# A reworked chain at the output product and the latents, and a head in pairs of row tiles

## The chip, the cores and the metric

The kernel runs on one core of a Trainium2 chip. The metric is device time in microseconds of one execution; lower is better. The engines named below are TensorE (PE), VectorE (DVE), ScalarE (ACT), GpSimd (POOL) and SyncE (SP, which issues transfers).

## The reference

One inference step of a decoder trunk with two layers, for 256 prompt tokens and 8 sample tokens (264 columns in all) with D = 1024. A layer is a SwiGLU block, a mixer and a second SwiGLU block, each behind an RMS norm. The mixer joins a gated short convolution with latent attention:

```python
yp = yp + 0.5 * swiglu(rmsnorm(yp, norm_ffn1[l]), w_ffn1_gate[l], w_ffn1_up[l], w_ffn1_down[l])
h = rmsnorm(yp, norm_mix[l])
b_g, u, qn, qp, ckv, kpe = mixer_project(h, w_in[l], q_a_norm[l], w_q_b[l], kv_a_norm[l], pos_p)
conv_y = b_g * short_conv(u_hist, conv_w[l], SEQ)
attn_o = prompt_mla(qn, qp, ckv, kpe, w_kv_b[l])
yp = yp + mixer_output(conv_y, attn_o, gn_conv[l], gn_attn[l], w_o[l])
yp = yp + 0.5 * swiglu(rmsnorm(yp, norm_ffn2[l]), w_ffn2_gate[l], w_ffn2_up[l], w_ffn2_down[l])
```

`mixer_output` normalises the convolution's 512 features and the attention's 512 features each by its own RMS and multiplies both with `w_o` (1024 x 1024). The sample group does the same with a paged cache of 1024 past positions. The FFN is 2816 wide. All inputs are float32.

## The kernel before

Features lie on the 128 partitions, tokens along the 264 columns, so D = 1024 is 8 tiles of rows, y[:, 0] to y[:, 7]. Every large weight comes as float32 in chunks of 256 columns and 8 row tiles (1 MB, tag "raw", 3 buffers) on SP's queue, and is split per unit of 128 columns into a high half (L231, a copy on ACT to fp32r) and a low half (L233, the rest, on DVE), each in two parts of 4 row tiles. There are 5 buffers for split units. `take()` hands the next split unit to the products, `done()` splits the next one; a chunk whose two units are split frees its buffer for the next load. A product of two split numbers is three matmuls (`mm3`, L250 high x high, L251 high x low, L252 low x high). `behind()` puts the low half on DVE behind the instruction last noted in `after[0]`.

The program is traced in one order, and a planner in the build orders the instructions of each engine by their place in the program and by when they become ready in its own model. So the order on an engine isn't always that of the text.

A norm goes like this: squares are summed in `ssA` or `ssB` over the row tiles; `sums` (L312) reduces that in blocks of 32 on DVE and adds over the partitions with a small matmul (L317); `rsqrt_of` (L298) is eight small operations of DVE; `over_rows` (L319) spreads the result over all rows by a transposition. `finish_y` (L329) makes the high and the low part of the next stage's right side `xg` from y (ACT and DVE) and the square's sum, on GpSimd in the output product except for the last tile.

The head (L995 to L1023) loads y in two halves of 4 row tiles (SP and ACT queue), the first weight chunk in two pieces and the next two chunks whole. Fifty matmuls on zeros or ones warm TensorE up; then xg for tiles 0 to 3, the first parts of units 0 and 1, xg for tiles 4 to 7, the second parts, and the squares, in between units 2 and 3. In the first FFN (`ffn`, `first`) units 0 and 1 (gate) run over all row tiles, then units 2 and 3 (up) with the norm's sums behind their first row tile, into the four "mm" banks of PSUM. Three banks bear the tag "x".

In the mixer (`mixer`) three generators are mixed by hand (ORDER): main (12 products of the projection, which give the convolution's four tiles z, each with high part h and low part lo), prompt (the latents, keys, queries and the eight heads) and sample (the cached attention). `latent` (L574) scales the latent (`ckvf`), splits it on ACT and DVE (`ckh`, `ckl`) and rotates the keys on GpSimd (`kp1`, `kp2`, `kpf`). A head's scores p, and their transposed copy pt, take a buffer of the tag "w" each (`wtile`, 4 buffers). `o_stats` (L933) reduces `ssA` (attention) and `ssB` (convolution) to two factors, `a_spread` (L947) scales and splits the attention's four tiles into `mg`, `c_spread` spreads the convolution's factor, and the output product runs row tile by row tile over four banks at once: row tiles 0 to 3 are the convolution's, 4 to 7 the attention's. `o_finish` (L961) evicts a bank (L963), adds to y (L964), splits the next unit and calls `finish_y`. Tiles 4 to 7 of the output follow one by one, then the second FFN.

## Time and profile before

| what | us |
|---|---|
| median of three runs | 1041.53 (1040.4 to 1047.66) |
| profiled execution | 1033.67 |
| its span, first to last instruction | 1031.9 |
| TensorE busy in the span | 1001.6 (97%) |
| DVE busy | 764.0 (74%) |
| ACT busy | 535.9 (52%) |
| GpSimd busy | 93.9 (9%) |

Times within the profile are counted from the span's start, in microseconds; mean durations are in nanoseconds where a row gives "mean ns". A row of the timeline gives start, duration, engine, line, operation, what it writes and reads, and in brackets how long the engine was idle before it and what ended the wait. An operation's duration overlaps the next one's start: matmuls of 264 columns take 0.28 and start every 0.12.

### The profile page before, as it was taken

The page shows a single profiled execution, that of the slowest core. Times are in us where ns is not written, and L with a number is a line of the kernel's source. Part 1 is how long each engine was busy: PE and PEld are TensorE (multiplying, and loading weights), DVE is VectorE, ACT ScalarE, POOL GpSimd, SP SyncE. Part 2 cuts the span into 40 slices and gives each one's busy share as a digit, 9 for nine tenths or more (in the row PEclk, how much of TensorE's full clock was granted, in tenths as well). Part 3 has the DMA queues.
Part 4 walks back from the last instruction along what each step waited for, and adds up shares of the span by engine and source line. Part 5 has one row for each costly group of instructions (what it writes and reads, how often), then busy time and mean ns, then how long its engine had stood idle before and what let it go on. Part 6 is the DMA issues. An engine that isn't in the chain of part 4 may idle for free.

```text
span 1031.9 us, 21616 instructions
## 1 busy us (share of the span) xinstructions
PE 1001.6 (97%) x8666; PEld 970.5 (94%) x8666; DVE 764.0 (74%) x1753; ACT 535.9 (52%) x1167; POOL 93.9 (9%) x135
## 2 busy tenths in 40 slices
PE   8999999999999999999999999999999899999996
PEld 7999999988788999999999999999878899999996
DVE  6988866689859877756688888566996897777452
ACT  6555445448636555545555555454674555555441
POOL 2110100030402000000001111000322100000000
PEclk9999999999999999999999999999999999999998
DMA  8867665535614755555566667454554265555531
GB/s 276 276 221 242 217 199 193 173 109 194 247 42 164 240 169 191 177 164 188 180 213 232 219 226 230 159 179 154 170 192 178 93 208 191 189 178 174 165 113 43
DMA packets 170787, 190.03 MB, mean 184 GB/s; under 512 B 3936, under 2 KB 163712, under 8 KB 170688
## 3 DMA queue, kind: packets, MB, share of 16 engines
q1 hardware_dynamic: 164048, 167.53, 49.7%
q0 software_dynamic: 5776, 19.49, 5.4%
q10 hardware_dynamic: 864, 1.64, 0.5%
q8 instruction: 68, 1.11, 0.4%
q14 instruction: 31, 0.25, 0.1%
HBM read 187.19 MB, written 1.49 MB: 183 GB/s over the span
## 4 chain that ended last, share of the span: by engine, by line
PE 85%; DVE 10%; ACT 3%; issue 1%; DMA 1%; ACTq 0%; SPq 0%; DVEq 0%
PE mm L250 27%; PE mm L252 27%; PE mm L251 26%; DVE lo L233 4%; PE x L779 1%; DVE y L964 1%; ACT hi L231 1%; DVE xg L332 1%; PE x L830 1%; DMA raw<-in_w_ffn_gate_dram 1%; PE x L694 1%; PE x L681 1%; DVE t L963 1%; ACT qg L635 0%; PE s L658 0%
## 5 line engine op out<-in xcount | busy, mean ns | idle before, releaser
L231 ACT ACTIVATE hi<-raw 128x512 fp32r<-128x512 f32 (+1 forms) x648 | 366.2, 612 | 367.3 <-PE mm L251 245.4
L233 DVE TENSOR_TENSOR lo<-raw,hi 128x512 fp32r<-128x512 f32 (+1 forms) x648 | 417.2, 677 | 112.2 <-ACT hi L231 102.7
L252 PE MATMUL mm<-xg,lo 128*128 128x264 f32 x1648 | 468.0, 284 | 7.1 <-DVE lo L233 7.0
L250 PE MATMUL mm<-xg,hi 128*128 128x264 f32 x1648 | 471.2, 286 | 2.4 <-DVE t L963 1.7
L251 PE MATMUL mm<-xg,hi 128*128 128x264 f32 x1648 | 467.4, 284 | 0.0
L252 PEld LDWEIGHTS mm<-xg,lo 128*128 128x128 f32 x1648 | 308.8, 188 | 10.6 <-DVE lo L233 9.6
L250 PEld LDWEIGHTS mm<-xg,hi 128*128 128x128 f32 x1648 | 310.5, 188 | 5.1 <-ACT hi L231 3.6
L251 PEld LDWEIGHTS mm<-xg,hi 128*128 128x128 f32 x1648 | 310.6, 188 | 0.2
L250 PE MATMUL mm<-act,hi 128*128 128x264 f32 x704 | 200.4, 285 | 0.0
L252 PE MATMUL mm<-act,lo 128*128 128x264 f32 x704 | 199.7, 284 | 0.0
L251 PE MATMUL mm<-act,hi 128*128 128x264 f32 x704 | 199.2, 283 | 0.0
L250 PEld LDWEIGHTS mm<-act,hi 128*128 128x128 f32 x704 | 132.3, 188 | 0.2 <-ACT t L1040 0.2
L252 PEld LDWEIGHTS mm<-act,lo 128*128 128x128 f32 x704 | 132.5, 188 | 0.0
L251 PEld LDWEIGHTS mm<-act,hi 128*128 128x128 f32 x704 | 132.4, 188 | 0.0
L464 POOL DMA_INDIRECT nat<-in_cache_ckv_dram,idx x32 | 33.4, 1044 | 445.7 <-DVE lo L233 189.7
L403 DVE TENSOR_TENSOR t<-mm,t 128x264 f32<-128x264 f32 x88 | 37.6, 427 | 40.1 <-PE mm L252 39.6
L394 DVE TENSOR_TENSOR t<-mm,Rw 128x264 f32<-128x264 f32 x88 | 37.6, 428 | 38.4 <-PE mm L252 38.4
L331 ACT ACTIVATE xg<-y,gains 128x264 fp32r<-128x264 f32 x48 | 24.1, 514 | 29.8 <-DVE y L449 19.1
L397 ACT ACTIVATE t<-t 128x264 f32<-128x264 f32 x88 | 36.3, 412 | 4.4 <-DVE t L394 4.3
L399 DVE SCALAR_TENSOR_TENSOR t<-t,t 128x264 f32<-128x264 f32 x88 | 37.6, 428 | 1.1 <-ACT t L397 1.1
L406 DVE TENSOR_TENSOR act<-t,act 128x264 fp32r<-128x264 f32 x88 | 37.7, 428 | 0.0
L405 ACT ACTIVATE act<-t 128x264 fp32r<-128x264 f32 x88 | 36.0, 409 | 0.7 <-DVE t L403 0.6
(230 smaller groups left out, 808.3 us busy)
## 6 DMA issues: line engine op xcount, KB each, us to landing
raw<-in_w_ffn_up_dram SPq DMA_DIRECT2D x44, 1024.0 KB, 5.2
raw<-in_w_ffn_gate_dram SPq DMA_DIRECT2D x43, 1024.0 KB, 5.2
raw<-in_w_ffn_down_dram SPq DMA_DIRECT2D x32, 1024.0 KB, 5.3
raw<-in_w_in_dram SPq DMA_DIRECT2D x14, 1024.0 KB, 5.4
raw<-in_w_ffn_down_dram SPq DMA_DIRECT2D x16, 768.0 KB, 4.6
raw<-in_w_o_dram SPq DMA_DIRECT2D x8, 1024.0 KB, 5.2
raw<-in_w_q_dram SPq DMA_DIRECT2D x2, 768.0 KB, 5.0
raw<-in_w_in_dram SPq DMA_DIRECT2D x2, 640.0 KB, 4.0
```

The costliest lines, as they stand in the source:

```text
L231: S.activation(h[:, k, f], raw[:, k, lo:hi][:, :, f], AF.Copy)
L233: V.tensor_tensor(r[:, k, f], raw[:, k, lo:hi][:, :, f], h[:, k, f].bitcast(F32), ALU.subtract)
L250: PE.matmul(ps, wh, xh, start=start, stop=False)
L251: PE.matmul(ps, wh, xl, start=False, stop=False)
L252: return PE.matmul(ps, wl, xh, start=False, stop=stop)
L394: V.tensor_tensor(g1, ps[:, :T], Rb, ALU.mult)
L397: S.activation(th, g1, AF.Tanh, scale=0.5)
L399: evac[0] = V.scalar_tensor_tensor(a1[m], th, 1.0, g1, ALU.add, ALU.mult).ins
L403: V.tensor_tensor(t, ps[:, :T], a1.pop(m), ALU.mult)
L405: S.activation(ah[:, m], t, AF.Copy)
L406: evac[0] = V.tensor_tensor(al[:, m], t, ah[:, m].bitcast(F32), ALU.subtract).ins
L464: G.indirect_dma_start(dst, None, src, bass.IndirectOffsetOnAxis(ap=idx[l][:, b:b + 1], axis=0))
```

## The change

At the output product: the last convolution tile (ct = 3) is squared on DVE into a tile of its own (`sqB`, a buffer of the tag "w" taken at the start of the mixer), ahead of the copy h and without ACT; the low part of that tile is made in `o_stats`, behind the reduction of `sqB`; the sums of `sqB` and of `ssB` (the other three tiles) are two matmuls into the same columns. `a_spread` scales its four tiles first, each followed by the high part on ACT, notes the last scaling in `after[0]`, and then makes the four low parts; it and `c_spread` are called behind row tile 1. The output product runs row tiles 0 to 3 over the four banks as before, and then row tiles 4 to 7 bank by bank, each with its `o_finish` behind it in the program.

At the latents: `ckh` is written by DVE straight from `kvg` and the factor, `ckvf` by a second DVE operation, and the rotation of the keys is on DVE, behind `ckl`. The additions of the squares of the heads and of `finish_y` go from GpSimd to DVE.

In the head: y comes in four pairs of row tiles, all on ACT's queue; the first weight chunk in four pieces of two row tiles; units 0 and 1 are split in four parts, and xg and the parts go in pairs of row tiles; units 2 and 3 are split next, then the squares. There are 34 warm-up matmuls. The two gate tiles of m = 2 go into banks of the tag "x".

```diff
-WARM = 50
+WARM = 34
@@ load_chunk
-        n = nk // 2 if i == 0 else nk
+        n = nk // 4 if i == 0 else nk
@@ split_steps
-            n = nk // 2
+            n = nk // 4 if i < 2 else nk // 2
             if n:
-                parts = [(slice(0, n), slice(0, w)), (slice(n, nk), slice(0, w))]
+                parts = [(slice(k, k + n), slice(0, w)) for k in range(0, nk, n)]
@@ trunk_kernel
-    nc.sync.dma_start(y[:, 0:4], a["xt"][:, 0:4])
+    for k in range(0, KT, 2):
+        nc.scalar.dma_start(y[:, k:k + 2], a["xt"][:, k:k + 2])
     load_chunk()
-    nc.scalar.dma_start(y[:, 4:8], a["xt"][:, 4:8])
     load_chunk()
@@ sums
-    def sums(ps, ss, c0=0):
+    def sums(ps, ss, c0=0, start=True, stop=True):
...
-        PE.matmul(ps[:, c0:c0 + NBLK], fold, q, start=True, stop=True)
+        PE.matmul(ps[:, c0:c0 + NBLK], fold, q, start=start, stop=stop)
@@ finish_y
-            (G if pool else V).tensor_tensor(ssA[:, :T], ssA[:, :T], sq[:, :T], ALU.add)
+            V.tensor_tensor(ssA[:, :T], ssA[:, :T], sq[:, :T], ALU.add)
@@ ffn
-                    ps = bank("mm")
+                    ps = bank("x" if first and m == 2 and not part else "mm")
@@ mixer
+        sqB = wtile(TP)
+        G.memset(sqB[:, T:TP], 0.0)
@@ latent
+            ckh, ckl = r264(), r264()
+            V.tensor_tensor(ckh, kvg, Rk[:, :T], ALU.mult)
             V.tensor_tensor(ckvf, kvg, Rk[:, :T], ALU.mult)
-            ckh, ckl = r264(), r264()
-            S.activation(ckh, ckvf, AF.Copy)
             after[0] = V.tensor_tensor(ckl, ckvf, ckh.bitcast(F32), ALU.subtract).ins
...
             with behind():
                 V.stream_shuffle(kp2[64:96, :T], kp1[64:96, :T], SWAP)
-            G.tensor_tensor(kp1[64:96, :T], kp1[64:96, :T], cos[64:96], ALU.mult)
-            G.tensor_tensor(kp2[64:96, :T], kp2[64:96, :T], sin[64:96], ALU.mult)
-            G.tensor_tensor(kpf[64:96], kp1[64:96, :T], kp2[64:96, :T], ALU.add)
+                V.tensor_tensor(kp1[64:96, :T], kp1[64:96, :T], cos[64:96], ALU.mult)
+                V.tensor_tensor(kp2[64:96, :T], kp2[64:96, :T], sin[64:96], ALU.mult)
+                V.tensor_tensor(kpf[64:96], kp1[64:96, :T], kp2[64:96, :T], ALU.add)
@@ h_out
-                G.tensor_tensor(ssA[:, 0:SEQ], ssA[:, 0:SEQ], sq, ALU.add)
+                V.tensor_tensor(ssA[:, 0:SEQ], ssA[:, 0:SEQ], sq, ALU.add)
@@ main, part 0, the last tile (ct = 3)
+                                V.scalar_tensor_tensor(sqB[:, :T], z, 1.0 / CD, z, ALU.mult, ALU.mult)
+                                S.activation(h, z, AF.Copy, scale=g)
+                                st["lo"] = lo, z, g, h
@@ o_stats
             sums(ps, ssA)
-            sums(ps, ssB, NBLK)
+            sums(ps, sqB, NBLK, start=True, stop=False)
+            lo, z, g, h = st["lo"]
+            V.scalar_tensor_tensor(lo, z, g, h.bitcast(F32), ALU.mult, ALU.subtract)
+            sums(ps, ssB, NBLK, start=False, stop=True)
@@ a_spread
+            fs = []
             for t in range(CT):
-                f = t264()[:, :T]
-                V.scalar_tensor_tensor(f, st["attn"][:, t], gain("gn_attn", 4 * l, t), Ra[:, :T], ALU.mult, ALU.mult)
-                S.activation(mg[0][:, t], f, AF.Copy)
-                V.tensor_tensor(mg[1][:, t], f, mg[0][:, t].bitcast(F32), ALU.subtract)
+                fs.append(t264()[:, :T])
+                after[0] = V.scalar_tensor_tensor(fs[t], st["attn"][:, t], gain("gn_attn", 4 * l, t), Ra[:, :T], ALU.mult, ALU.mult).ins
+                S.activation(mg[0][:, t], fs[t], AF.Copy)
+            for t in range(CT):
+                V.tensor_tensor(mg[1][:, t], fs[t], mg[0][:, t].bitcast(F32), ALU.subtract)
@@ the output product
-        for k in range(KT):
+        for k in range(CT):
             for w, ps in zip(us, pss):
                 o_part(ps, w, k)
-            if k == 2:
+            if k == 1:
                 a_spread()
-            if k == 5:
                 c_spread()
-            if k == 5:
                 c_store()
         for m in range(4):
+            for k in range(CT, KT):
+                o_part(pss[m], us[m], k)
             o_finish(m, pss[m])
@@ the head
-    for kt in range(4):
-        finish_y(kt, gain("norm_ffn1", 0, kt), square=False)
     two = [split_steps(), split_steps()]
-    for half in range(3):
+    for half in range(4):
+        for kt in (2 * half, 2 * half + 1):
+            finish_y(kt, gain("norm_ffn1", 0, kt), square=False)
         for u in two:
             next(u, None)
...
+    for u in two:
+        next(u, None)
+    split_unit()
+    split_unit()
     for kt in range(KT):
...
+        finish_y(kt, None, split=False)
```

## Rows read from the trace of the kernel before

**Rows 1.** The page, part 1: engine, busy us, share, instructions.
```profile
PE 1001.6 (97%) x8666; PEld 970.5 (94%) x8666; DVE 764.0 (74%) x1753; ACT 535.9 (52%) x1167; POOL 93.9 (9%) x135
```

**Rows 2.** Waits of TensorE, whole span: engine, line, releaser, total us, times, longest.
```profile
PE mm L252 <- DVE lo L233: 7.0, 8, 1.7
```

**Rows 3.** Timeline, output product of layer 0: start, us, engine, line, operation, [idle].
```profile
292.11 0.43 DVE L901 TENSOR_TENSOR t<-t,mm 128x264 f32<-128x264 f32 x1 [0.24 <-PE mm L252]
293.05 0.50 ACT L905 ACTIVATE r<-t,gains 128x264 fp32r<-128x264 f32 x1
294.45 0.48 DVE L316 TRANSPOSE_TENSOR_REDUCE sm<-ssB 128x9 f32<-128x288 f32 x1
295.42 0.17 DVE L939 TENSOR_SCALAR sm<-x 128x9 f32<-128x9 f32 x1 [0.48 <-PE x L317]
297.92 0.68 DVE L233 TENSOR_TENSOR lo<-raw,hi 128x512 fp32r<-128x512 f32 x1
299.48 1.29 DVE L953 SCALAR_TENSOR_TENSOR t<-attn,gains,w 128x264 f32<-128x264 f32 x3
300.47 0.76 PE L250 MATMUL mm<-qg,hi 128*128 128x264 f32 x4 [1.96 <-ACT qg L954]
307.26 0.80 DVE L963 TENSOR_TENSOR t<-mm,Rw 128x264 f32<-128x264 f32 x2 [4.13 <-PE mm L252]
```

**Rows 4.** Stretches, layer 0: length, busy (x in it) by engine, clock, DMA, GB/s.
```profile
300.00:304.00 4.00, 3.53 (x18) 3.38 (x19) 2.63 (x7) 1.65 (x4) 0.00 (x0) 0.69 0.02 4
302.00:304.00 2.00, 2.00 (x11) 2.00 (x11) 0.64 (x2) 0.42 (x1) 0.00 (x0) 0.50 0.04 8
316.00:320.00 4.00, 4.00 (x35) 4.00 (x35) 4.00 (x8) 2.82 (x6) 1.30 (x2) 1.00 0.78 255
320.00:324.00 4.00, 3.14 (x23) 2.69 (x22) 4.00 (x8) 2.27 (x5) 0.81 (x1) 1.00 0.37 109
324.00:328.00 4.00, 2.92 (x23) 2.63 (x22) 3.96 (x9) 1.26 (x4) 0.94 (x1) 1.00 0.47 164
```

**Rows 5.** Timeline: an addition of layer 0, and the output product of layer 1.
```profile
313.53 0.98 DVE L964 TENSOR_TENSOR y<-y,t 128x264 f32<-128x264 f32 x1
...
803.75 0.75 PE L250 MATMUL mm<-qg,hi 128*128 128x264 f32 x4 [1.96 <-ACT qg L954]
...
809.02 0.80 DVE L963 TENSOR_TENSOR t<-mm,Rw 128x264 f32<-128x264 f32 x2 [2.61 <-PE mm L252]
```

**Rows 6.** Timeline of the latents, layer 0.
```profile
222.75 0.49 PE L606 MATMUL mm<-hi,r 128*128 128x512 f32 x1 [0.33 <-ACT r L580]
225.01 1.17 POOL L596 TENSOR_TENSOR t<-t,con 32x264 f32<-32x264 f32 x1
227.00 2.05 DVE L233 TENSOR_TENSOR lo<-raw,hi 128x512 fp32r<-128x512 f32 x2
```

**Rows 7.** Timeline of the head.
```profile
1.54 7.10 PE L999 MATMUL s<-ssB 128*128 128x256 bf16 x50 [1.54 <-DVE one L992]
8.25 1.15 ACT L231 ACTIVATE hi<-raw 128x512 fp32r<-128x512 f32 x2 [1.86 <-DMA raw<-in_w_ffn_gate_dram]
18.36 0.39 PE L252 MATMUL mm<-xg,lo 128*128 128x264 f32 x1 [1.66 <-DVE lo L233]
19.78 0.36 PE L317 MATMUL x<-sm,fold 128*128 128x9 f32 x2 [0.20 <-DVE sm L316]
```

**Rows 8.** Head: a stretch, as rows 4, and an issue from 2.25: count, KB, us to landing.
```profile
10.00:11.00 1.00, 1.00 (x9) 0.82 (x8) 1.00 (x4) 1.00 (x4) 0.00 (x0) 1.00 1.09 346
...
raw<-in_w_ffn_up_dram SPq DMA_DIRECT2D x1, 1024.0 KB, 10.4
```

**Rows 9.** Heads of layer 0: users of "w" (ns min/median/max, first to last start); timeline.
```profile
L665 DVE CUSTOM_DVE_ANT_0 w<-s,tri,sm x8: 349/406/478, 251.6 to 274.6; 128x128 f32<-128x128 f32 x4, 128x256 f32<-128x256 f32 x4
L684 DVE COPY w<-x x8: 546/557/558, 258.0 to 284.5; 128x384 f32<-128x384 f32 x8
...
287.55 0.74 POOL L704 TENSOR_TENSOR ssA<-ssA,t 128x256 f32<-128x256 f32 x1 [2.17 <-ACT t L703]
```

More of the change, by code (lines that the diff above doesn't have):

```diff
@@ L904, in main @@
                             h, lo = r264(), r264()
-                            S.activation(h, z, AF.Copy, scale=g)
-                            if ct == 0:
-                                S.activation(ssB[:, :T], z, AF.Square, scale=CD ** -0.5)
-                            else:
-                                sq = t264()[:, :T]
-                                S.activation(sq, z, AF.Square, scale=CD ** -0.5)
-                            V.scalar_tensor_tensor(lo, z, g, h.bitcast(F32), ALU.mult, ALU.subtract)
-                            if ct:
-                                V.tensor_tensor(ssB[:, :T], ssB[:, :T], sq, ALU.add)
+                            if ct < CT - 1:
+                                S.activation(h, z, AF.Copy, scale=g)
+                                if ct == 0:
+                                    S.activation(ssB[:, :T], z, AF.Square, scale=CD ** -0.5)
+                                else:
+                                    sq = t264()[:, :T]
+                                    S.activation(sq, z, AF.Square, scale=CD ** -0.5)
+                                V.scalar_tensor_tensor(lo, z, g, h.bitcast(F32), ALU.mult, ALU.subtract)
+                                if ct:
+                                    V.tensor_tensor(ssB[:, :T], ssB[:, :T], sq, ALU.add)
+                            else:
+                                V.scalar_tensor_tensor(sqB[:, :T], z, 1.0 / CD, z, ALU.mult, ALU.mult)
+                                S.activation(h, z, AF.Copy, scale=g)
+                                st["lo"] = lo, z, g, h
                             zh.append(h)
@@ L936, in o_stats @@
             sums(ps, ssA)
-            sums(ps, ssB, NBLK)
+            sums(ps, sqB, NBLK, start=True, stop=False)
+            lo, z, g, h = st["lo"]
+            V.scalar_tensor_tensor(lo, z, g, h.bitcast(F32), ALU.mult, ALU.subtract)
+            sums(ps, ssB, NBLK, start=False, stop=True)
             v = small(2 * NBLK, tag="v2")
@@ L1000, in trunk_kernel @@
     open_xg()
-    for kt in range(4):
-        finish_y(kt, gain("norm_ffn1", 0, kt), square=False)
     two = [split_steps(), split_steps()]
-    for half in range(3):
+    for half in range(4):
+        for kt in (2 * half, 2 * half + 1):
+            finish_y(kt, gain("norm_ffn1", 0, kt), square=False)
         for u in two:
             next(u, None)
-        if half == 0:
-            for kt in range(4, KT):
-                finish_y(kt, gain("norm_ffn1", 0, kt), square=False)
-    hi = t264()[:, :T]
+    for u in two:
+        next(u, None)
+    split_unit()
+    split_unit()
     for kt in range(KT):
-        acc = hi if kt >= 4 else ssA[:, :T]
-        if kt % 4 == 0:
-            S.activation(acc, y[:, kt], AF.Square, scale=D ** -0.5)
-        else:
-            sq = t264()[:, :T]
-            S.activation(sq, y[:, kt], AF.Square, scale=D ** -0.5)
-            (V if kt >= 4 else G).tensor_tensor(acc, acc, sq, ALU.add)
-        if kt == 3:
-            split_unit()
-    V.tensor_tensor(ssA[:, :T], ssA[:, :T], hi, ALU.add)
-    split_unit()
+        finish_y(kt, None, split=False)
     def setup_rest():
```

## The prediction

> **What bounds the kernel.** I read the page first: TensorE is busy for 97% of the span [rows 1], and in a full stretch of 4 us it has 35 matmuls of 264 columns in flight or begun [rows 4], one start every 0.12 us. So time is won only where TensorE stands still. Next I read TensorE's waits, where DVE's low halves of weights lead with 7.0 us [rows 2], then looked for the places in the timeline, and last counted matmuls by stretch. There are three places: the output product of each layer with the start of the FFN behind it [rows 3 to 5], the latents [rows 6] and the head [rows 7]. In rows 4 the reader should see that at the output product of layer 0 a stretch has 18 matmuls, and two later ones 23 each, where a full one has 35.
>
> **The chain at the output product.** In layer 0 DVE's last product z starts at 292.11. Its copy h waits on ACT behind weight halves and ends at 293.55; the square follows it on ACT, then an addition, and the reduction of the squares starts at 294.45. The first operation on the sums, L939, is at 295.42, the first scaled attention tile (L953) at 299.48, with two weight halves on DVE in between, and TensorE, out of work since 298.4, goes on at 300.47 after 1.96 idle [rows 3]. I count 2.1 from start to start, and the same in layer 1 [rows 5].
> The change squares z on DVE itself: 0.43 for z and 0.43 for one more operation (L953's three take 1.29), and the reduction starts near 293.0, not 294.45. The older sums are reduced separately, long since ready; should that come second it costs 0.4. I take 1.1 for what L939 moves forward. If instead the second reduction queues behind the low half of z, which needs h at 293.55, only 0.45 is won. The two weight halves between L939 and L953 (0.6 each by spacing) now come behind the four scalings, since `after` is set there: 1.2 more. So L953 starts near 297.2, and with the 0.99 from L953 to the first product as today, TensorE can go on at 298.2, just as it runs out. The four subtractions now follow four scalings (0.41 each by spacing), so the first low half is there near 299.2; four high products of 0.12 cover all but 0.3. Taken: 0.3 of the 2.1 stays, **1.8 won in each layer, 3.6**; bounds 1.2 and 2.1 each. One more small pair of matmuls, for the second sum, costs TensorE 0.2 to 0.36 (L317 in rows 7): **+0.4** in both layers.
> In layer 0 the clock falls behind this gap: granted 0.50 in 302 to 304, that is 1.2 GHz, with 11 matmuls [rows 4]. From the restart to the first eviction layer 0 takes 307.26 - 300.47 = 6.8, layer 1 809.02 - 803.75 = 5.3 [rows 3, 5]. No gap, no fall: **1.5 won**; bounds 0 and 1.7 (12 missing matmuls and rounding).
>
> **The order of the products behind it.** Today the four banks finish together; DVE waits 4.13 for the first eviction at 307.26 [rows 3] and then is full, 4.00 of every 4.00 to 324 [rows 4], while TensorE comes to wait for it: 2 x (35 - 23) x 0.12 = 2.9 us, layer 1 alike. The change ends bank 0 after 12 of its own matmuls, near 300.7. DVE's work per tile is an eviction, an addition, two weight halves and a low half of xg: 0.35 + 0.35 + 1.2 + 0.41 by spacing. GpSimd's sums run beside it, and DVE's addition takes 0.98 there [rows 5], not 0.43: 0.55 lost for each of six sums in a layer. A sum on DVE costs 0.35 to 0.43 and takes that loss away; nothing gained, I say, and 0.4 each if the loss stayed. So 8 x 2.7 = 21 us of DVE work start some 6 us earlier and end near 321, while TensorE's 144 products need 17.3 from 298.7 and want the FFN's first weights from 316 to 320. I take 2.4 of the 2.9: **4.8 in two layers**; bounds 1.5 and 2.9 each, since the first four tiles give DVE 2.7 of work for 1.45 of TensorE and part of the wait may move to the banks.
>
> **The latents.** ckh comes from DVE, 0.43 of work there, and no longer by way of ACT; TensorE's wait for it of 0.33 goes. The rotation of the keys leaves GpSimd (1.17 each) for three DVE operations, at most 0.43 each like an operation on all 128 rows, ahead of the weight halves: 1.05 later for these. But two halves that take 2.05 beside GpSimd [rows 6] take 2 x 0.6 without it, and more before them are slowed alike. Taken: 0.4 per layer, **0.8 won**; bounds -0.5 and +1. The sums of the heads' squares go from GpSimd (0.74 [rows 9]) to DVE, mostly when it is free; nothing, and 0.4 each without that cover.
>
> **The head.** The first 512 KB of weights are there at 8.25, the warm-ups end at 1.54 + 7.10 = 8.64, the products start behind both; a low half stops them until 18.36, and the sums come at 19.78 [rows 7]. The transfers run at 346 GB/s, and the up-weights land 10.4 after their issue, at 12.6 [rows 8]. In the change the first pair of y and the first 256 KB of weights, 0.53 MB, and the gains are there after some 2.2 of start and 0.6/0.346 = 1.7, near 4.5 with the landing; the others follow every 1.5. ACT and DVE just keep pace: two xg and two halves of half width per pair, between 1.4 and 1.9 each. The first 48 products then end near 12. But the up-weights come no sooner, the same bytes being ahead of them: their four ACT halves (0.57 each) end near 15.0, DVE's third at 15.1, and the stream is whole from there, not from 18.36: 3.2 at most for this, 4 with the wait at the sums. The squares come behind the splits in the program; if they run there, TensorE waits for the sums until 18.5 and almost nothing is won. Bounds 0 and 4, taken **2.5**. Sixteen fewer warm-ups end before the data and are no time. The four issues on ACT's queue end before y lands: nothing, or 0.45 each. Two more banks for the opening tiles keep TensorE from waiting for evictions: no gain of their own; without them up to 1 us of the 2.5 would be lost.
> The Trainium skill, DMA: Bandwidth & Descriptors, Rules for kernel authors, asks for 1 MiB or more per transfer and says that spreading over queues adds no bandwidth. By that rule the head's first data come little sooner; the sum would be 9.3 in place of 11.8. No run here shows pieces of 256 KB yet.
>
> **The buffer.** The square's tile holds one of the four `w` buffers for the whole mixer, so the heads' p and transposed copies share three. Today the first head takes 258.0 - 251.6 = 6.4 from p to its copy, and copies come every (284.5 - 258.0) / 7 = 3.8 [rows 9]. A last p that waits for a buffer comes later by their difference, 2.6. The heads' last sum is written at 288.3 [rows 9] and wanted by the new chain near 292.5: 4 us of slack. I take **+0.5 per layer, +1.0**; bounds 0 and 14 each (below).
>
> **The sum.** -3.6 + 0.4 - 1.5 - 4.8 - 0.8 - 2.5 + 1.0 = -11.8. The profiled execution took 1033.67 (span 1031.9): 1021.9. The median shown, 1041.53, is 0.76% higher; on its scale 1041.53 x 1021.9 / 1033.67 = **1029.7**. About 1%, 10.4 us, is what a measurement of this kernel can tell from no change: the forecast is only just over it.
>
> **The rivals.**
> *The head gives nothing.* The up-weights set its end, and the sums wait for the squares. For it: rows 8; against: ACT is free while it waits for the up-weights and could square then. Without the 2.5: 1024.4, or 1032.1 on the median's scale. TensorE has some 3 us with few products there; a fall of the clock as in layer 0 would make it 1033.6, though equal gaps gave a fall in layer 0 and none in layer 1. The Trainium skill, TensorE: Matmul & The Clock Gate, What's actually happening, has the slow clock as the default that activity lifts; by that rule fewer warm-ups and the thin stretch speak for the fall.
> *DVE stays the limit.* The wait before the FFN only moves to the banks and the 4.8 are not won: 1026.7, or 1034.5. For it: DVE at 4.00 of 4.00 [rows 4].
> *The chain does not shorten.* A planner orders the instructions; if it puts the second reduction behind h, gap and fall stay: 1027.0, or 1034.8.
> *Slower: the heads starve for buffers.* Place: 251.6 to 284.5 in layer 0 and its like. Heads strictly in a row take 8 x 6.4 = 51 in place of 33, 18 more, less 4 of slack: 14 per layer, so 1033.7 - 12.8 + 28 = 1048.9, or 1056.9. It decides from a delay of 10.4 per layer (6.4 + 4). Against it: a p is free as soon as it is transposed, and main products stand by for TensorE.
>
> **Chances.** Forecast 0.56 (own range 1025 to 1034), head 0.18, DVE 0.14, chain 0.08, buffers 0.04. Three quarters of the first and a quarter of the next two lie under 1031.1: faster by over 1% 0.50, within 1% 0.45, slower 0.05. Range 1022 to 1038: below, the bounds of chain, order and head together; above, the three middle rivals with some delay of the heads.
>
> **What would show it.** Right: no wait over 0.5 at L250 for qg, no half clock near 300, the output product's first eviction 6 us ahead of its fourth, 33 or more matmuls in each 4 us up to the FFN, the head's stream whole from 15. Wrong: TensorE waiting for the sums near 16 to 18, for evictions of the last tiles before the FFN, or heads that wait while DVE idles.

## Result and profile after

| what | before | after |
|---|---|---|
| timed executions, median (lowest to highest) | 1043.08 us (1040.40 to 1048.99, 7) | 1034.93 us (1033.56 to 1038.17, 7) |
| profiled execution (span) | 1033.67 us (1031.9) | 1035.09 us (1033.3) |
| mean granted clock of TensorE in it | 0.995 | 0.992 |

The ratio is 0.9925, with a 95% interval of 0.9902 to 0.9947: faster by 0.75%, some 8 us. The forecast was 1029.7, with a range of 1022 to 1038. One thing must be explained at once: in the two profiled executions, after is 1.4 us *longer*. The profiled execution of before is 7 to 15 us under all its timed ones, that of after lies among its timed ones. On which chip that profile of before was taken isn't on record. So the two traces can't be subtracted as they stand; they are read stage by stage.

The page of after, part 1, and TensorE's waits (columns as in [rows 1, 2]):

```profile
PE 1003.9 (97%) x8654; PEld 973.0 (94%) x8654; DVE 766.5 (74%) x1788; ACT 534.4 (52%) x1167; POOL 73.2 (7%) x110
...
PE x L815 <- issue: 8.1, 8, 1.2
...
PE mm L252 <- DVE lo L233: 1.6, 3, 0.7
...
PE mm L250 <- ACT qg L967: 1.3, 2, 0.7
```

The low halves for which TensorE waited 7.0 us [rows 2] are down to 1.6, and the gap at qg (the views' name for the high parts `mg[0]` of the scaled attention tiles) from 1.96 a layer [rows 3, 5] to 0.65. The line of L815 is new: 8.1 us in which TensorE waits for nothing that the profile shows, at the small matmuls of the paged heads.

The output product of layer 0, timeline (as [rows 3]) and stretches of TensorE alone (length, busy time with the number of matmuls, granted clock, busy share of the transfer engines, GB/s):

```profile
298.30 0.43 DVE L904 TENSOR_TENSOR t<-t,mm 128x264 f32<-128x264 f32 x1 [0.32 <-PE mm L252]
298.77 0.43 DVE L920 SCALAR_TENSOR_TENSOR w<-t 128x264 f32<-128x264 f32 x1
...
301.32 0.17 DVE L951 TENSOR_SCALAR sm<-x 128x9 f32<-128x9 f32 x1 [0.66 <-PE x L317]
...
304.45 1.71 DVE L966 SCALAR_TENSOR_TENSOR t<-attn,gains,w 128x264 f32<-128x264 f32 x4
305.45 0.75 PE L250 MATMUL mm<-qg,hi 128*128 128x264 f32 x4 [0.67 <-ACT qg L967]
308.20 0.43 DVE L977 TENSOR_TENSOR t<-mm,Rw 128x264 f32<-128x264 f32 x1
...
308.00:312.00 4.00, 4.00 (x35) 1.00 0.01 4
...
320.00:324.00 4.00, 4.00 (x35) 1.00 0.49 162
```

From z to the first scaled tile it takes 304.45 - 298.30 = 6.15 us, where before it took 7.37 [rows 3]; the first eviction comes 2.75 after TensorE's restart, not 6.8; the clock stays whole, and 35 matmuls stand in each 4 us from 308 to 328, where before two such stretches had 23 [rows 4]. This stage went much as forecast, though the wait for qg, 0.67, is over the 0.5 that the prediction named as a sign of being right. But it begins 6 us later than before (z at 298.30, not 292.11), and the time was lost ahead of it, in the heads:

```profile
268.14 0.35 PE L815 MATMUL x<-con,ws 128*32 128x32 f32 x16
...
271.90 0.28 PE L815 MATMUL x<-con,ws 128*32 128x32 f32 x4 [1.18 <-issue]
273.36 0.78 PE L815 MATMUL x<-con,ws 128*32 128x32 f32 x36 [1.17 <-issue]
```

These are 61 of the 64 small matmuls of `s_turn`, 0.9 us of work in one piece in the profile of before. Here they come in portions of 16, 2, 3, 4 and 36, the last ones 1.4 us apart. At the same time GpSimd's eight gathers of the paged values (L465) fill the transfer engines (354 GB/s from 266 to 270 us, 409 from 270 to 274). I call this *the stall*, and measure it by how much longer than without it TensorE takes from the first product of the heads' scores to the last one of the paged heads.

The head of after (timeline, as [rows 7]):

```profile
13.45 2.19 ACT L231 ACTIVATE hi<-raw 128x512 fp32r<-128x512 f32 x4 [1.32 <-DMA raw<-in_w_ffn_up_dram]
...
20.93 0.36 PE L317 MATMUL x<-sm,fold 128*128 128x9 f32 x2 [0.44 <-DVE sm L316]
24.27 0.39 PE L252 MATMUL x<-xg,lo 128*128 128x264 f32 x1 [1.67 <-DVE lo L233]
```

The sums come 1.15 later than before (19.78, [rows 7]), after a stream that is whole from 15 us; behind them TensorE waits 1.67 for a low half that is behind the norm on DVE.

### The profile page after: what moved, and what is told of

Its sections match the earlier page's. It is cut to its first block, busy times and chain, and to the rows that moved or that the text cites. A ratio compares the mean times of both kernels' runs of the same rounds, so it can differ in the third digit from the quotient of the medians.

```text
span 1033.3 us, 21600 instructions
## 1 busy us (share of the span) xinstructions
PE 1003.9 (97%) x8654; PEld 973.0 (94%) x8654; DVE 766.5 (74%) x1788; ACT 534.4 (52%) x1167; POOL 73.2 (7%) x110
## 4 chain that ended last, share of the span: by engine, by line
PE 87%; DVE 7%; ACT 2%; DMA 2%; issue 1%; ACTq 0%; DVEq 0%
PE mm L250 27%; PE mm L252 27%; PE mm L251 27%; DVE lo L233 2%; PE x L782 1%; DMA raw<-in_w_ffn_up_dram 1%; PE x L697 1%; PE x L833 1%; PE x L684 1%; ACT hi L231 1%; DMA raw<-in_w_in_dram 1%; PE x L815 0%; PE s L661 0%; DVE t L966 0%; ACT qg L638 0%
## 5 line engine op out<-in xcount | busy, mean ns | idle before, releaser
L231 ACT ACTIVATE hi<-raw 128x512 fp32r<-128x512 f32 (+2 forms) x652 | 367.0, 610 | 362.7 <-PE mm L251 238.5
L233 DVE TENSOR_TENSOR lo<-raw,hi 128x512 fp32r<-128x512 f32 (+2 forms) x652 | 413.3, 668 | 112.6 <-ACT hi L231 103.3
L251 PE MATMUL mm<-xg,hi 128*128 128x264 f32 x1632 | 464.4, 285 | 0.0
L251 PEld LDWEIGHTS mm<-xg,hi 128*128 128x128 f32 x1632 | 308.6, 189 | 0.3
L251 PE MATMUL mm<-act,hi 128*128 128x264 f32 x704 | 199.2, 283 | 0.0
L251 PEld LDWEIGHTS mm<-act,hi 128*128 128x128 f32 x704 | 132.4, 188 | 0.0
L465 POOL DMA_INDIRECT nat<-in_cache_ckv_dram,idx x32 | 33.5, 1048 | 482.7 <-DVE lo L233 228.3
```

Of the source, the lines that this page charges most:

```text
L231: S.activation(h[:, k, f], raw[:, k, lo:hi][:, :, f], AF.Copy)
L233: V.tensor_tensor(r[:, k, f], raw[:, k, lo:hi][:, :, f], h[:, k, f].bitcast(F32), ALU.subtract)
L251: PE.matmul(ps, wh, xl, start=False, stop=False)
L465: G.indirect_dma_start(dst, None, src, bass.IndirectOffsetOnAxis(ap=idx[l][:, b:b + 1], axis=0))
```

## Experiments

Twelve kernels ran in three groups, each group on a chip of its own, beside the kernel before. Its median was 1041.8 in the first group, 1036.2 in the second and 1035.4 in the third: that chips differ is part of the answer. All edits are against the changed kernel, except for c0 and f2.

### First group: whose is the stall?

**c0_before** is the kernel before, unchanged, with a new profile.

> The kernel before, unchanged, profiled once more. Its first profiled execution took 1033.67 us, while its timed executions took 1040 to 1049. Theory A (the stutter of TensorE at the small transposing matmuls of the paged heads, L815 of after, comes and goes from execution to execution with the gathers' transfers): a second profiled execution should be near 1040 to 1045 and show matmul groups at that line (L812 of before) with waits named issue, some 5 to 8 us per layer. Theory B (the stutter belongs to the changed kernel alone, because its heads share three w buffers): this profile shows none, is within 2 us of 1033.7, and the 7 to 15 us up to the timed executions lie elsewhere.

Measured: 1044.75 us, span 1043.0. In layer 0 (timeline) and in two stretches of TensorE:

```profile
269.43 0.43 DVE L785 TENSOR_REDUCE sm<-x 128x1 f32<-128x257 f32 x1 [3.21 <-PE x L694]
269.96 0.51 ACT L675 ACTIVATE w<-w,sm 128x256 f32<-128x256 f32 x1 [3.14 <-DVE sm L785]
270.81 0.53 PE L681 MATMUL x<-con,w 128*128 128x128 f32 x3 [2.50 <-DVE sm L785]
275.34 0.60 PE L812 MATMUL x<-con,ws 128*32 128x32 f32 x35 [0.74 <-issue]
...
266.90:270.90 4.00, 1.50 (x13) 1.00 0.99 340
270.90:274.90 4.00, 3.70 (x46) 0.57 1.00 404
```

So before has the stall too: DVE, ACT and TensorE stand for 2.5 to 3.2 us, and the clock falls to 0.57 behind it. DVE's L785 waits for a product of TensorE (L779) that had begun at 263.99 and lasted 2.38; the signal that it was done came 3 us late. From the first scores to the paged heads' last product (L850) it takes 46.3 and 47.8 us in the two layers here, 41.9 and 42.9 in the first profile. That first profile had nearly escaped the stall, and the prediction was made on it. Its 1033.7 lies in the range of before's timed executions in the second and third groups (1032.8 to 1039.8), so it may have come from such a chip.

**e1_own_tile** gives the heads their fourth buffer back:

```diff
-    R2 = stat.tile([P, T], F32, name="R2")
+    R2f = stat.tile([P, TP], F32, name="R2"); V.memset(R2f[:, T:TP], 0.0); R2 = R2f[:, :T]
-        sqB = wtile(TP)
-        G.memset(sqB[:, T:TP], 0.0)
+        sqB = R2f
```

> The changed kernel with the square of z in R2 (widened to 288 columns), which is dead at that place, so that the heads have four w buffers again; all else as in after. Theory B (three buffers delay the heads): the heads' copies come from 257 to 284 as before, their last sum at 288, 6 us earlier than in after in each layer, and the time falls by 6 to 12 us, to 1023 to 1029. Theory A (an instruction transfer of TensorE falls into the gathers): the heads may shift a little, the waits named issue at L815 stay near 8 per layer in some profile, and the time is within 2 us of after, 1033 to 1037.

Measured: 1034.17 (1031.60 to 1034.53), ratio 0.9915 (0.9897 to 0.9932). The heads take 49.0 and 48.3, as in after (49.2 and 48.3). The missing buffer isn't the stall's cause. What it does cost lies elsewhere (f3, below).

**e2_warm50** has the warm-ups of before:

```diff
-WARM = 34
+WARM = 50
```

> The changed kernel with 50 warm-up matmuls as before in place of 34. The 16 more matmuls end at about 8.6 us and delay the first products by 1.2 us at most (7.2 to 8.6), so the head itself gives at most 1.4 back; but they move TensorE's instruction transfers 32 instructions ahead in the rest of the program. Theory A: the transfer at 270.6 moves to about 269 or earlier, out of the small matmuls or deeper into them, and the waits named issue change by more than 3 us in at least one layer; the time changes by -10 to +5. Theory B: the waits at that place stay within 1 us of after's, and the time is after's plus 0 to 1.4, 1035 to 1036.5.

Measured: 1034.19 (1033.88 to 1034.48), ratio 0.9924 (0.9909 to 0.9939). Sixteen more warm-up matmuls cost nothing, and the stall is as long: 7.8 us named issue at L815, heads of 49.0 and 48.2. So theory A in that form, by which the stall hangs on where TensorE's instruction transfers fall, is not borne out.

**e3_head_before** has the head of before: pieces, loops, warm-ups and banks, each as the change's diff shows it removed. Its core:

```diff
-        n = nk // 4 if i == 0 else nk
+        n = nk // 2 if i == 0 else nk
...
-                    ps = bank("x" if first and m == 2 and not part else "mm")
+                    ps = bank("mm")
...
-    for half in range(4):
-        for kt in (2 * half, 2 * half + 1):
-            finish_y(kt, gain("norm_ffn1", 0, kt), square=False)
+    for kt in range(4):
+        finish_y(kt, gain("norm_ffn1", 0, kt), square=False)
```

> The changed kernel with the head of before (weights and y in the old pieces, 50 warm-ups, squares shared with GpSimd, one bank kind for the opening tiles); the latents, the heads' squares, the chain and the order at the output product as in after. By the marks of the two profiles the new head is worth 0.5 us (first matmul of the rotary keys 213.5 before, 213.0 after): the time should be that of after plus 0.5, 1035.4, give or take 1. If the new head is worth the 2.5 that the prediction put on it: 1037.4. If the new head costs something later (other places of the instruction transfers): below after's, 1028 to 1033.

Measured: 1036.81 (1036.35 to 1037.78), ratio 0.9949 (0.9933 to 0.9964), 2.6 us over e1 and e2 on the same chip. The new head is worth what the prediction put on it, 2.5; the 0.5 by the marks (first instructions of a stage) of the two profiles was misleading, since the same head differs by up to 1.8 from execution to execution (first product of the rotary keys at 212.0 to 213.8 in nine profiles with the new head, 213.5 to 215.1 in four with the old one; their means differ by 1.5). With the new head this mark follows the landing of the up-weights: in eight of the nine profiles it comes 199.6 after ACT's first half of them, which waits for the landing and begins at 12.4 to 13.8 (e1 has 200.9). The stall is as in after (7.8 at its line L814).

### Second group: the gathers, the order, the chain

**e4_two_in_flight** spaces the gathers:

```diff
             for b in range(4):
+                if len(sent) >= 2:
+                    G.tensor_copy(seen[:, 0:1], sent[-2])
                 gather(nat[:, b].rearrange("p t c -> p (t c)"), "cache_ckv", l, 4 * s + b)
+                sent.append(nat[:, b, 0, 0:1])
...
-                            G.memset(u[:, 0:2], 0.0)
+                            V.memset(u[:, 0:2], 0.0)
```

> The changed kernel, but GpSimd starts a gather of the paged values only when the gather two before it has landed (a copy of one landed column by GpSimd stands between them), and the two zero columns ahead of u are written by VectorE, so that nothing waits behind GpSimd. Every byte still moves. Theory A (the eight gathers back to back hold up TensorE's signals and instructions): the stall of 6 to 8 us behind 268 in layer 0 and its like in layer 1 shrinks to under 2, from the first scores to the paged heads' last product it takes 42 to 44 us in place of 48 to 49, and the time falls by 8 to 13, to 1021 to 1027. Theory A with a bad trade: the gathers now take over 24 us, so that the products that read them (L833, from 283 in after) wait and half of that is lost, 1027 to 1031. Rival (the stall has nothing to do with the gathers, or exists in profiled executions alone): within 2 us of 1034.5.

Measured: 1038.72 (1036.25 to 1044.67), ratio 1.0029 (1.0010 to 1.0047): a little slower than before. No wait named issue is left, but the gathers come too late, and TensorE waits for them 4.7 us a layer:

```profile
PE x L837 <- DMA nat<-in_cache_ckv_dram,idx: 9.4, 4, 3.9
```

In and behind these waits the clock falls (0.50 from 282 to 286, 0.70 from 286 to 290). The first four gathers took 4.4 to 7.3 us from issue to landing, and two or three in flight don't fill the transfer engines (206 GB/s from 270 to 274, 406 in the same stretch of e6). The copy had no tie to the gather behind it, and the planner put it one gather later, so that up to three were under way. The bad trade was foreseen, its size wasn't (1027 to 1031 expected); and since the stall is short on this chip anyway (e6, e7), there was little to gain.

**e5_four_gathers** leaves out the second four gathers of a layer; its second four sequences are averaged over the first four's values:

```diff
-            nat = keep.tile([P, 4, NSLOT, KV], F32, tag="B", bufs=2, name=nm("nat"))
-            for b in range(4):
+            nat = st["nat", 0] if s else keep.tile([P, 4, NSLOT, KV], F32, tag="B", bufs=2, name=nm("nat"))
+            for b in range(4 - 4 * s):
```

> The changed kernel without the second four of the eight gathers of each layer's paged values: the second four sequences are averaged over the values of the first four, 2.1 MB per layer are not moved. Theory A: the gathers end near 267 in layer 0, before the small matmuls at 268; the stall there shrinks from 6 to 8 us to under 2 per layer, the granted clock stays whole there, and the time is 1020 to 1027. Rival (the stall comes from those small matmuls themselves or from where TensorE's instructions are loaded): they still show waits named issue of 3 us or more per layer and the time stays over 1031.

Measured: 1020.96 (1020.60 to 1021.34), ratio 0.9858 (0.9836 to 0.9881). There is no wait named issue, the heads take 41.8 in both layers, and the mean clock is 0.996. But on this chip kernels with all eight gathers (e6, e7) hardly stall either, so alone it doesn't show the cause.

**e6_order_before** takes the products in the old order:

```diff
-        for k in range(CT):
+        for k in range(KT):
...
-            if k == 1:
+            if k == 2:
                 a_spread()
+            if k == 5:
                 c_spread()
+            if k == 5:
                 c_store()
         for m in range(4):
-            for k in range(CT, KT):
-                o_part(pss[m], us[m], k)
             o_finish(m, pss[m])
```

> The changed kernel with the order of the products of before at the output product: the first four banks take all eight k together, so that they end together. The prediction put 4.8 us on this order in two layers: the time should be 1039 to 1039.5, with 30.4 from the first scaled attention tile to the first eviction of the second FFN in place of 28.0, and waits for evictions (L250 behind t) of over 2 us per layer back. Rival (DVE stays the limit in either order, the new chain alone ends the wait): within 1.5 us of after, 1033 to 1036.

**e7_chain_before** has the old chain: z squared on ACT behind its copy, one reduction, each subtraction behind its scaling, no tile for the square.

```diff
-            sums(ps, sqB, NBLK, start=True, stop=False)
-            lo, z, g, h = st["lo"]
-            V.scalar_tensor_tensor(lo, z, g, h.bitcast(F32), ALU.mult, ALU.subtract)
-            sums(ps, ssB, NBLK, start=False, stop=True)
+            sums(ps, ssB, NBLK)
...
-            for t in range(CT):
-                V.tensor_tensor(mg[1][:, t], fs[t], mg[0][:, t].bitcast(F32), ALU.subtract)
```

> The changed kernel with the chain of before: z squared on ACT behind its copy, one reduction of all the squares, the four subtractions each behind its scaling, no tile of its own for the square. The order of the products, the head and the latents as in after. By the prediction the chain with its clock fall is worth 3.6 + 1.5 - 0.4 and costs 1.0 for the buffer: 1034.5 + 3.7 = 1038.2, with TensorE waiting for qg some 2 us in each layer. Rival 1 (the gap is as long in both, since the first product of the attention half now follows the fourth scaling of DVE later): 1034 to 1035.5. Rival 2 (the missing w buffer costs as much as the chain brings): 1033 to 1035 with the heads 2 us shorter.

Measured: e6 1025.19 (1024.15 to 1027.16), ratio 0.9903 (0.9884 to 0.9922); e7 1024.57 (1024.31 to 1028.99), ratio 0.9900 (0.9878 to 0.9921). The absolute expectations fell, since the stall is short here. The two are read in the stage itself, together with f1 and f2.

### Third group: the change with and without the stall

**f0_after** is the changed kernel, **f1_after_four** is it with the edit of e5, **f2_before_four** is the kernel before with the same edit.

> The changed kernel, unchanged, beside the three below on one chip. Theory (the change is worth 11 to 12 us by its own steps, and the heads' stall during the gathers, which differs between executions, chips and kernels, decides what is left): where this chip's stall is long (6 us and more per layer in the profile) the time is 1033 to 1036, where it is short, 1020 to 1026; the ratio to before lies between 0.984 and 0.994. Rival (the steps are worth only 8): the ratio is 0.992 to 0.993 whatever the stall.

> The changed kernel without the second four gathers of each layer's paged values (their four sequences are averaged over the first four's values): after without the stall. 1020.5 to 1021.5, with no wait named issue at L815, L833 or L836. If the stall is caused by the gathers, after itself on this chip is longer by what its profile shows as stall; if not, both are equally long.

> The kernel before without the second four gathers of each layer's paged values (the same part left out): before without the stall. The difference to the one above is the change without the stall. Theory: 11 to 12 us more than after without four, 1031.5 to 1033.5. Rival (the steps are worth 8): 1028.5 to 1029.5. Before itself, with eight gathers, should be longer by the stall in it, some 3 to 10.

Measured: f0 1023.01 (1021.97 to 1024.40), ratio 0.9884 (0.9861 to 0.9907); f1 1020.72 (1020.33 to 1021.85); f2 1033.80 (1032.50 to 1035.92). Without the stall the change is worth 1033.80 - 1020.72 = 13.1 us, a little more than the 11 to 12 expected. With all gathers it is worth 12 on this chip.

Both f1 and f2 are free of waits named issue, so here the traces can be subtracted. The first instructions of the stages of layer 0, in f2 and then in f1 (timeline):

```profile
214.58 1.10 PE L526 MATMUL mm<-y,wg 128*32 128x264 f32 x16
247.54 0.82 PE L658 MATMUL s<-kg,qg 96*128 96x128 f32 x4
288.82 0.64 PE L850 MATMUL x<-olT,wuv 128*64 128x8 f32 x16
300.49 1.23 ACT L954 ACTIVATE qg<-t 128x264 fp32r<-128x264 f32 x3 [6.14 <-DVE t L953]
```

```profile
212.06 1.10 PE L527 MATMUL mm<-y,wg 128*32 128x264 f32 x16
244.36 0.82 PE L661 MATMUL s<-kg,qg 96*128 96x128 f32 x4
286.18 0.64 PE L853 MATMUL x<-olT,wuv 128*64 128x8 f32 x16
296.61 1.63 ACT L967 ACTIVATE qg<-t 128x264 fp32r<-128x264 f32 x4 [5.23 <-DVE t L966]
```

The last mark is the first product of the second FFN's down weights that DVE takes up (465.3 and 457.3 in layer 0, 967.0 and 953.8 in layer 1). Differences of f1 to f2 by stage:

| stage | layer 0 | layer 1 | predicted, both |
|---|---|---|---|
| start to the rotary keys (head) | -2.5 | | -2.5 |
| rotary keys to first scores (latents) | -0.65 | -0.65 | -0.8 |
| first scores to L850 (heads) | +0.55 | +0.6 | +1.0 |
| L850 to the first qg, and from there to the FFN's down product | -1.2 - 4.0 | -1.2 - 4.0 | -3.6 + 0.4 - 1.5 - 4.8 = -9.5 |

The sum is -13.2, the spans differ by 1032.0 - 1018.6 = 13.4. Now the stage that gives most, in stretches of TensorE that begin 2 us ahead of the first qg (L954, L967): f2, f1, e7 and e6, layer 0 and, of f2 and e7, layer 1 (in f1 and e6 it is alike within 2 matmuls).

```profile
298.50:302.50 4.00, 2.05 (x14) 0.96 0.00 0
302.50:306.50 4.00, 4.00 (x23) 0.62 0.02 4
...
320.50:328.50 8.00, 6.07 (x43) 1.00 0.47 145
...
804.20:808.20 4.00, 4.00 (x23) 0.61 0.02 4
822.20:830.20 8.00, 6.07 (x44) 1.00 0.49 146
```

```profile
294.60:298.60 4.00, 2.98 (x22) 1.00 0.00 0
298.60:302.60 4.00, 4.00 (x35) 1.00 0.02 4
...
316.60:324.60 8.00, 8.00 (x68) 1.00 0.70 233
```

```profile
296.10:300.10 4.00, 2.04 (x15) 1.00 0.00 0
300.10:304.10 4.00, 4.00 (x23) 0.57 0.02 4
318.10:326.10 8.00, 8.00 (x68) 1.00 0.73 239
...
797.50:801.50 4.00, 2.05 (x15) 1.00 0.00 0
801.50:805.50 4.00, 4.00 (x34) 1.00 0.02 4
819.50:827.50 8.00, 8.00 (x67) 1.00 0.67 229
```

```profile
297.30:301.30 4.00, 2.98 (x23) 1.00 0.00 0
301.30:305.30 4.00, 4.00 (x35) 1.00 0.02 4
319.30:327.30 8.00, 8.00 (x64) 1.00 0.77 254
```

From one matmul's start to the next's it is 8.00 / 68 = 0.118 us. The 14 us between the last two stretches hold 117 and 118 matmuls in all of them. From f2 to f1 the gap shrinks by 8 matmuls (0.9 us), the fall of the clock behind it by 12 (1.4 us, in *both* layers), the wait ahead of the FFN by 25 (2.9 us): 5.3 a layer. e7 shows that the gap is the chain's (x15 with the old chain), and that the same gap is followed by half a clock in layer 0 and by none in layer 1. e6 shows that the old order by itself costs 4 of 68 matmuls, 0.5 us, and 5 of 67 in layer 1 (x62), 0.6: not the 2.4 a layer that the prediction put on it.

**f3_own_tile_squares** has the edit of e1, and in the head

```diff
+    for kt in range(4):
+        finish_y(kt, None, split=False)
     split_unit()
     split_unit()
-
-    for kt in range(KT):
+    for kt in range(4, KT):
         finish_y(kt, None, split=False)
```

> The changed kernel with the square of z in R2 (four w buffers for the heads) and with the squares of the first four row tiles of y ahead of the two up-weights' halves, in the 1.3 us in which ACT waits for these weights. The sums of the first norm come 1.0 to 1.4 earlier (19.5 to 20 us in place of 20.9), the low half that TensorE waits for behind them too, so that 1 to 1.5 of the head is won; the own tile gives 0 to 1. Time: that of after on this chip less 1 to 2. Rival (the up-weights' halves come later by what the squares take, and the head is as long): within 0.5 of after.

Measured: 1019.35 (1018.76 to 1024.49), ratio 0.9860 (0.9835 to 0.9884): the fastest of all that compute everything, 3.7 under f0 by the medians, 2.5 by the ratios. The head's mark comes 1.8 earlier (L527's first product at 211.2, not 213.0):

```profile
12.07 1.04 ACT L339 ACTIVATE t<-y 128x264 f32<-128x264 f32 x3
13.15 2.19 ACT L231 ACTIVATE hi<-raw 128x512 fp32r<-128x512 f32 x4
...
19.15 0.36 PE L317 MATMUL x<-sm,fold 128*128 128x9 f32 x2 [0.23 <-DVE sm L316]
22.50 0.39 PE L252 MATMUL x<-xg,lo 128*128 128x264 f32 x1 [0.70 <-DVE lo L233]
```

Four squares fill ACT's wait for the up-weights, these come no later (their halves at 13.15; 13.46 in f0), and the sums come 1.8 earlier. Of this, 0.3 is that these halves begin earlier, as they do from execution to execution; counted from them the sums come after 6.0 us, in f0 and f1 after 7.5: the squares give 1.5. The own tile gives 0.6 at the chain in each layer (9.85 from L853 to the first qg in e1 and f3, 10.44 in f0), and this is why (DVE, f0 and then f3, layer 0):

```profile
292.89 0.48 DVE L316 TRANSPOSE_TENSOR_REDUCE sm<-w 128x9 f32<-128x288 f32 x1
293.43 0.49 DVE L948 SCALAR_TENSOR_TENSOR r<-t,gains,r 128x264 fp32r<-128x264 f32 x1
293.84 0.47 DVE L316 TRANSPOSE_TENSOR_REDUCE sm<-ssB 128x9 f32<-128x288 f32 x1
```

```profile
290.22 0.48 DVE L316 TRANSPOSE_TENSOR_REDUCE sm<-R 128x9 f32<-128x288 f32 x1
290.62 0.44 DVE L316 TRANSPOSE_TENSOR_REDUCE sm<-ssB 128x9 f32<-128x288 f32 x1
290.98 0.45 DVE L948 SCALAR_TENSOR_TENSOR r<-t,gains,r 128x264 fp32r<-128x264 f32 x1
```

In after the planner puts z's low half ahead of the older sums' reduction; in f3 the two reductions stand together, and the sums leave 0.5 earlier.

## Why the prediction was right, and where it wasn't

The direction held: 1.1% was forecast (1029.7 of 1041.53), 0.75% was measured in the runs of the result and 1.2% in the third group. By its own chances the favourite, faster by over 1% (0.50), didn't come in the runs of the result; within 1% (0.45) did. The prediction called some 1% the least that a measurement can tell from no change; the interval here, 0.2% to either side, told 0.75%. By its own sum, 1021.9 on the scale of the profiled execution, it fits f0 (1023.0) and f1 (1020.7), both on a chip where the stall is short. That the sum of 11.8 is so near to the 13.2 of the stages is in part luck: the chain gave 1.4 less than its 3.2, the clock 1.3 more and the wait ahead of the FFN 1.0 more than was put on them, the last without need of the edit that it was ascribed to.

*The step that failed is the last one, the scale.* The prediction took the 0.76% between the profiled execution and the median for a factor. It was the stall: some 8 us in the heads of before, of which its first profile had little (0.6 and 1.6 over the 41.3 of f2), while the profile of after had all of it. By the stage from the first scores to L850 (L853) the stall is 48.7 (mean of the two layers in after, e1, e2 and e3) - 41.8 (f1) = 6.9 a layer. The same kernel, as after and as f0, has spans of 1033.3 and 1021.3, and its heads take 49.2 + 48.3 and 42.8 + 42.6, 12.1 less: the stall is all of the difference between these two executions. For before it is 1041.8 - 1033.8 = 8.0 in both layers together by the medians of the first group and of f2, for after 1034.2 (e1, e2) - 1020.7 = 13.5. So 5.5 of the 13.1 are given back to a longer stall, and 7.6 are left, close to the result's 8.1. These are medians from different chips; the one profile of before on the first chip, c0, has heads 11.6 longer than f2's, but that execution was 3.0 over the group's median. Why the changed kernel stalls longer isn't settled: the buffer, the warm-ups and the head don't do it (e1, e2, e3). Among what wasn't undone on that chip are the DVE operations that were GpSimd's in the latents and at the heads' squares; this wasn't tried. That the gathers have a part in the stall is supported, but not proven where it is long: it falls in their time, at their pace (one portion per 1.4 us, eight gathers of 0.5 MB at 400 GB/s take 1.3 each), and with half of them it is gone; but the runs with half of them were on chips where it is short (f1 is 2.3 under f0, f2 1.6 under before). Nor are the gathers enough: f0, the same kernel as after, moves them as fast (405 GB/s from 270 to 274, 409 in after) and hardly stalls. What the first chip adds to them is open.

*The gap at the output product.* Predicted 1.8 won, less 0.2 for the third sum; measured 0.9 in the count of matmuls. The step that was mis-sized is the reduction: the text named the case in which the second one comes behind z's low half and only 0.45 is won, and took 1.1 for it. The planner did just that: in after the first operation on the sums (L951) comes 3.02 behind z, where L939 came 3.31 behind it, so 0.3 was won there. The two weight halves put behind the scalings gave 0.9, not 1.2. Of these 1.2 together TensorE loses 0.3 again to the wait for the first low half (L251 for qg, 0.7 in two layers). L966 comes 6.15 after z where 297.2 - 292.11 = 5.1 was reckoned.

*The clock.* Predicted 1.5, in layer 0 alone, as the trace of before had it; in f2 and in c0 it falls in both layers, so that 2 x 1.4 was there to win. The Trainium skill, TensorE: Matmul & The Clock Gate, What's actually happening, calls the slow clock the default that activity lifts. The runs agree in kind (0.57 to 0.62 of the full clock in the 4 us behind the long gap in f2 and in layer 0 of e7, 1.00 wherever the gap is short), but equal gaps (x15 twice in e7) gave 0.57 once and 1.00 once: one layer of one trace was too little to count falls by.

*The order of the products.* The wait ahead of the FFN went, and by more than predicted (2 x 2.9, not 4.8), but the order wasn't needed for it: with the new chain the old order costs 1.1 in two layers (e6), and with the old chain the new order keeps TensorE full just as well (e7). With either of the two undone the wait is nearly or wholly away. What e6 and e7 have in common against before in this stage is the sum of squares on DVE. In f2 the additions and low halves beside GpSimd's sums took 0.63 and 0.61 on the mean, in e6 0.43 and 0.49: 2.6 us a layer for eight of each, as much as the six sums cost on DVE. So the balance of nothing that the prediction gave this edit holds for DVE's time, and how much of the wait it removed was not separated.

*The latents* gave 1.3 in place of 0.8, inside their bounds. *The buffer.* The heads' stage is 1.1 longer in f1 than in f2, near the 1.0 taken for the buffer, but that the buffer does it isn't shown: with a tile of its own the heads are no shorter in e1 (49.0 and 48.3, in after 49.2 and 48.3), where the stall is long, and take 41.9 and 43.1 in f3, in f0 42.8 and 42.6. What the tile is seen to cost is the 0.6 a layer at the chain.

*The head* gave 2.5 by the marks of f1 and f2, 2.6 by the medians of e3 and 1.5 by the mean of the marks: 2.5 was predicted. The medians of e3 weigh most, since the marks scatter with the landing of the up-weights. Its mechanism was right, and so was the doubt: the squares do come behind the splits (ACT waits 1.32 for the up-weights and squares only then), and f3 wins 1.5 by moving four of them. The Trainium skill, DMA: Bandwidth & Descriptors, Rules for kernel authors, asks for 1 MiB or more per transfer; pieces of 256 KB moved no less here (355 GB/s from 2 to 8 us, where before had 351 with its larger ones), and the sum by that rule, 9.3, is further from the 13.1 than the 11.8.

*The rivals.* The head did give; DVE didn't stay the limit; the chain shortened by half of what was said; the heads didn't starve for buffers. What did slow the heads, the stall, was in none of them, since the one profile hardly showed it.

## What to carry to other kernels

Before a profiled execution is used as the base of a sum, compare it with the timed ones: if it is well outside their range, take a second profile and find the stage that differs, since the difference needn't carry over as a factor. When several edits aim at one wait, undo each by itself: the first may already have removed it. A wait of an engine for a transfer is a place for work that is wanted soon after, if that work's inputs are already there.

## What the runs showed of the hardware

- While eight gathers of 0.5 MB ran back to back (350 to 410 GB/s in stretches of 4 us), a signal of TensorE came 3 us late (c0) and its small matmuls came in portions with up to 1.2 us of waiting between them (after). In every profile of the first group's chip (c0, e1 to e3) and in after, the heads were longer by 5.0 to 7.5 us per layer than with half of the gathers; on two other chips, with all eight back to back, by 0 to 3. The weights of the head, at 346 GB/s [rows 8], came without it.
- The same kernel before took 1041.8, 1036.2 and 1035.4 us (medians) on three chips, the changed one 1034.2 (e1, e2, nearly the same) on the first and 1023.0 on the third: the gain from one change was 0.75% and 1.2%.
- Equal gaps of TensorE ahead of the output product were followed by half the clock in one layer and by the whole clock in the other, in e7 and in the first profile of before (1.96 us idle in both layers, [rows 3, 5]).
- How long the new head took went with the landing of the up-weights: the rotary keys' first product came 199.6 us after ACT's first half of them in eight of nine profiles, and that half began at 12.4 to 13.8 us.
